# A residual gate's terms moved from three engines to GpSimd, and its closing matmul done by split products

## The chip, the cores and the metric

The kernel runs on one core of one Trainium2 chip. The metric is device time in microseconds (us) of one execution, the median of three runs. Five queues of instructions run side by side on the core: PE (TensorE, with PEld its weight loads), DVE (VectorE), ACT (ScalarE), POOL (GpSimd) and SP (SyncE, which issues most of the transfers). Each runs its own instructions in order; semaphores tie them together.

## The reference

One layer of a hybrid encoder over 1024 tokens of width 1024, in fp32:

```python
mod = silu(c) @ w_ada + b_ada                  # shift, scale, gate: 1024 each
u = layer_norm(x) * (1 + scale) + shift
h = u @ w_in                                   # q, k, v, g of 8 FoX and 8 stick-breaking heads
y_fox = fox_attention(...) * silu(fg)          # softmax with a forget bias, causal
y_sb = stick_breaking_attention(...) * silu(sg)
y = concat([y_fox, y_sb]) @ w_out
out = layer_norm(2**0.25 * x + gate * y, ln_g, ln_b)
```

Only `gate` matters here: `gate = silu(c) @ w_ada[:, 2048:] + b_ada[2048:]`, a vector of 1024 numbers. Value heads and `w_out` are drawn with a smaller scale (DeepNorm).

## The kernel before, in words

Products that need fp32 accuracy are split: a number is its fp32r part (hi) plus the rest (lo), and three fp32r matmuls (hi·hi, hi·lo, lo·hi) stand for one fp32 matmul. The weights are read from HBM in pieces of 128x512 (`raw`) and split on POOL by `fetch_w`: a TENSOR_SCALAR makes hi (L125), a TENSOR_TENSOR subtraction makes lo (L126).

The heads run in 8 pairs. The program begins with the first projections of pairs 0 and 1 (q, k, g of pair 0, q and k of pair 1): a first pass over tokens 0 to 511 and then a second pass over tokens 512 to 1023 (the loops at L740 and L752), eight blocks `kb` of 128 input channels each, accumulated in PSUM. `late_round` turns and rounds the inputs of the second pass. `evac_m` empties an accumulator: ACT casts, DVE subtracts, and for keys (`evac_k`) SP copies the head's half across partitions by DMA (L243). The last accumulator of the second pass is `st_k1b`, keys of pair 1.

After that attention goes unit by unit: a unit is a pair p, a head h and a query block i. `att_scores` multiplies queries and keys (S, L411 and L412, one buffer); for stick-breaking heads ACT makes two sigmoids out of it (`kp`, `be`, L431 and L432), DVE runs a cumulative product over `kp` (the scan, L437 and L441), POOL multiplies (L445). Two units later `att_transpose` turns `be` (T, L462), and ACT and DVE split the result (`pt`, L464 and L465). `att_pv` multiplies by the values (L477). Between these PE works through a list of fillers, first the remaining value tiles of pairs 0 and 1 (`v_tile`, L311 to L313) and the g projection of pair 1.

The gate: the 1024 rows of its weight come in eight tiles `wg` of 128x1024 (`load_gate`), in the buffers of the tag `att` (six of them, shared with inputs `x`, with `kp` and `be`, and with the bias tile `bg`). `gate_term` scales a tile by silu(c) of its rows (`sc`) and adds it to `gate`, in two halves of 512 columns. Here ACT makes the first term and scales the left halves, POOL adds these, and DVE does the right halves in one instruction. `gen_gate` then adds up the 128 partitions by a plain fp32 matmul with a matrix of 0.5 and adds half of the bias (DVE, L717). It runs beside the first fillers and waits GATE of their steps. The result is used only much later, when POOL multiplies it into `w_out` (L123).

What sets the order: PE and, in the start, SP run in the order in which the program text issues them. ACT, DVE and POOL are ordered by a planner, which places each instruction when its own clock says that it can run; buffers of a tag go to the next tile when their last reader is done. So where the text issues the gate's work decides the order of SP and, through the planner, that of the others.

Of the kernel before, what the change touches and what calls it, by code (L numbers as in the profile page):

```python
# [8 lines left out]
F32 = mybir.dt.float32  # L9
F32R = mybir.dt.float32r  # L10
AF = mybir.ActivationFunctionType
ALU = mybir.AluOpType

P = 128
SEQ = 1024
D = 1024
NB = 8
# [10 lines left out]
def tile_hybrid_layer(  # L28
# [17 lines left out]
    nc = tc.nc  # L46

    cp = ctx.enter_context(tc.tile_pool(name="const", bufs=1))
# [4 lines left out]
    def big(tag, bufs, name, dt=F32, shape=None):  # L53
        return sb.tile(shape or [P, 1024], dt, tag=tag, bufs=bufs, name=name)

    def att_tile(name, dt=F32):
        return big("att", 6, name, dt)

    def pt_tile(which, name, dt=F32R, shape=None):
        return big("pth" if which == 0 else "ptl", 3, name, dt, shape)  # L60

    def acc_tile(name):
        return ps.tile([P, 512], F32, tag="acc", bufs=2, name=name)
# [4 lines left out]
    def t_tile(name):  # L68
        return ps.tile([P, 512], F32, tag="T", bufs=2, name=name)
# [3 lines left out]

    RING = 5
    WARM = (4, 1, 1, 1, 1)
    GEARLY = 8
    NORM_ON = {6: nc.vector, 7: nc.vector}
    FROW = 12
    SPACE = 5
    GATE = 6  # L80

    def after(*instructions):
        stack = ExitStack()
        for i in instructions:
            stack.enter_context(tc.issue_after(i.ins))
        return stack
# [7 lines left out]
                            channel_multiplier=1, compare_op=ALU.is_ge, fill=MASKED)  # L94
    ones = cp.tile([P, 1], F32, tag="ones", name="ones")
    nc.gpsimd.memset(ones, 1.0)
    half = cp.tile([P, 1], F32, tag="half", name="half")
    nc.gpsimd.memset(half, 0.5)

    qz = [[cp.tile([P, P], F32R, tag=f"qz{h}{b}", name=f"qz{h}{b}") for b in range(2)] for h in range(2)]  # L100
    for h in range(2):
# [2 lines left out]
    gate = cp.tile([P, D], F32, tag="gate", name="gate")  # L104
# [8 lines left out]
    def raw_tile(name):  # L113
        return sb.tile([P, 528], F32, tag="wraw", bufs=2, name=name)

    def ring_w(key):
        return [sb.tile([P, 528], F32R, tag=tag, bufs=RING, name=f"{tag}_{key}") for tag in ("whi", "wlo")]

    def fetch_w(key, src, n, scale=None, home=None):
        raw = raw_tile(f"raw_{key}")[:, :n]  # L120
        nc.sync.dma_start(raw, src)
        if scale is not None:
            nc.gpsimd.tensor_tensor(raw, raw, scale, op=ALU.mult)  # L123
        hi, lo = home or ring_w(key)
        nc.gpsimd.tensor_scalar(hi[:, :n], raw, 1.0, 1.0, op0=ALU.mult, op1=ALU.mult)  # L125
        nc.gpsimd.tensor_tensor(lo[:, :n], raw, hi.bitcast(F32)[:, :n], op=ALU.subtract)  # L126
        return hi, lo
# [30 lines left out]
    sc = cp.tile([P, NB], F32, tag="sc", name="sc")  # L158
# [3 lines left out]
    for kt in range(NB):  # L162
        nc.tensor.matmul(sc_all[:, kt // 4, kt % 4 * P:][:, :P], sc[:, kt:kt + 1].to_broadcast([P, P]), ident,
                         start=True, stop=True)
# [52 lines left out]
    def u_round(kb, a=0, b=512):  # L217
        full = xT[kb, a][:, :b - a]
        nc.scalar.activation(u_hi[kb][:, a:b], full, AF.Identity, scale=modc[:, kb, 0:1], bias=modc[:, kb, 1:2])
        return nc.scalar.activation(full, full, AF.Identity, scale=modc[:, kb, 0:1], bias=modc[:, kb, 1:2])  # L220
# [340 lines left out]
    def start_steps(ns, accs, kb, a=0, b=512, parts=(0, 1)):  # L561
        s = slice(a, b)
        w = {}
        for n in ns:
            hi, lo = split[("k", kb) if n < NW else ("h", kb // 4)]
            at = n if n < NW else kb % 4
            w[n] = hi[:, at * P:at * P + P], lo[:, at * P:at * P + P]
        if 0 in parts:
            for n in ns:
                nc.tensor.matmul(accs[n], w[n][0], u_hi[kb][:, s], start=(kb == 0), stop=False)  # L570
                nc.tensor.matmul(accs[n], w[n][1], u_hi[kb][:, s], start=False, stop=False)
        if 1 in parts:
            for n in ns:
                nc.tensor.matmul(accs[n], w[n][0], u_lo[kb][:, s], start=False, stop=(kb == NB - 1))
# [36 lines left out]
    rounded = u_round(0)  # L611
# [14 lines left out]
    v0_w, v0_raw = {}, {}  # L626
# [63 lines left out]
    wg = {}  # L690

    def load_gate(kt):
        wg[kt] = att_tile(f"wg_{kt}")
        nc.sync.dma_start(wg[kt], w_gate[kt])

    def gate_term(kt, h):
        s = slice(h * 512, h * 512 + 512)
        if kt == 0:
            nc.scalar.activation(gate[:, s], wg[kt][:, s], AF.Copy, scale=sc[:, 0:1])
        elif h == 0:  # L700
            nc.scalar.activation(wg[kt][:, s], wg[kt][:, s], AF.Copy, scale=sc[:, kt:kt + 1])
            nc.gpsimd.tensor_tensor(gate[:, s], gate[:, s], wg[kt][:, s], op=ALU.add)
        else:
            nc.vector.scalar_tensor_tensor(gate[:, s], wg[kt][:, s], sc[:, kt:kt + 1], gate[:, s],
                                           op0=ALU.mult, op1=ALU.add)

    def gen_gate():
        b = att_tile("bg")
        nc.sync.dma_start(b, b_gate.to_broadcast([P, D]))
        for _ in range(GATE):  # L710
            yield
        for h in range(2):
            s = slice(h * 512, h * 512 + 512)
            gp = t_tile(f"gate_{h}")

            nc.tensor.matmul(gp, half.to_broadcast([P, P]), gate[:, s], start=True, stop=True)
            nc.vector.scalar_tensor_tensor(gate[:, s], b[:, s], 0.5, gp, op0=ALU.mult, op1=ALU.add)  # L717
            yield

    def late_round(kb):  # L720
        u_turn(kb, 512, 1024)
        return u_round(kb, 512, 1024), u_rest(kb, 512, 1024)
# [13 lines left out]
    rounded = late_round(1)  # L736
# [3 lines left out]
    for kb in range(NB):  # L740
        if kb + 2 < NB:
            rounded = late_round(kb + 2)
        start_steps(range(2), acc1, kb, 512, 1024)
        if kb < 4:
            load_gate(kb)
        if kb < len(evacs):
            n, h = evacs[kb]
            with after(*rounded):
                evac_m(*START[n], 0, acc0[n], (h,))
    acc1 += [pv_tile("st_g0b", True), pv_tile("st_q1b"), acc_tile("st_k1b")]  # L750
    v0_w.update((n, fetch_w(f"v0_{n}b", w_v[0, n], 512)) for n in (2, 3))
    for n in range(5):  # L752
        if n >= 2:
            for kb in range(NB):
                start_steps((n,), acc1, kb, 512, 1024)
                step = (n - 2) * NB + kb
                if step % 3 == 1 and step // 3 < GEARLY:
                    with after(*rounded):
                        gate_term(step // 3, 0)
                        gate_term(step // 3, 1)  # L760
                    if step // 3 < 4:
                        load_gate(step // 3 + 4)
        last_evac = evac_m(*START[n], 1, acc1[n])
        if n == 2:
            floor.append(ps.tile([P, 512], F32, tag="fl", bufs=1, name="floor"))
            nc.vector.memset(floor[0][:, :512 - P], 0.0)
            nc.scalar.copy(floor[0][:, 512 - P:], ident)
# [184 lines left out]
    for k in range(len(units) + LAG + 1):  # L952
        if k < len(units):
# [12 lines left out]
            p, h, i = units[k]  # L966
# [85 lines left out]
```

## Time and profile before

| | us |
|---|---|
| median of 3 runs | 694.79 |
| lowest, highest | 694.29, 694.94 |
| the profiled execution | 694.61 |
| its span, first to last instruction | 692.6 |
| PE busy in the span | 674.5 (97%) |
| DVE, ACT, POOL busy | 462.3, 384.3, 410.1 |

The profiled execution took 694.61 us, of which 692.6 us lie between the first and the last instruction; some 2.0 us are around it. The granted TensorE clock was 0.996 on average. In the profile's rows a line number is that of the kernel before, a name is a tile's with the buffer numbers left out, and what stands in brackets is the idle time ahead of an instruction and what ended it.

### The profile page before, as it was taken

Reading aid. Unit: us, or ns where it says so; the run is one execution under the profiler, and the core shown is the slowest. Engines: PE = TensorE matmul, PEld = TensorE weight load, DVE = VectorE, ACT = ScalarE, POOL = GpSimd, SP = SyncE. Lnnn points to the kernel's source line nnn. Section 1 sums busy time; section 2 is a strip of 40 time slices with the busy share of each in tenths; the row PEclk is TensorE's granted clock in tenths of the full one; section 3 lists DMA queues with packets and bytes.
Section 4 is the critical chain, followed back from the end, with each engine's and each line's share of the span. In section 5 each row is a group of like instructions: output and inputs, shape, how many; then the busy total and the mean of one; then the engine's idle time right before and its main releaser. Section 6 shows DMA issues by size and latency. Waiting matters only on the chain.

```text
span 692.6 us, 11784 instructions
## 1 busy us (share of the span) xinstructions
PE 674.5 (97%) x4033; PEld 589.2 (85%) x4033; DVE 462.3 (67%) x930; ACT 384.3 (55%) x866; POOL 410.1 (59%) x532
## 2 busy tenths in 40 slices
PE   7999999999999999999999999999999999999995
PEld 4789888888998888889998888889988889888884
DVE  5985668776656676767576665666565667774644
ACT  4666557766658576666675564655565667521000
POOL 4560477565439565556388897877584364655422
PEclk9999999999999999999999999999999999999998
DMA  8953351102102112112044553454341298153301
GB/s 308 415 228 129 95 196 55 28 23 55 54 9 70 41 48 60 38 46 62 12 142 156 176 161 114 146 159 145 100 130 58 75 293 339 58 170 108 118 31 61
DMA packets 44027, 81.59 MB, mean 118 GB/s; under 512 B 5120, under 2 KB 18880, under 8 KB 43072
## 3 DMA queue, kind: packets, MB, share of 16 engines
q1 hardware_dynamic: 42816, 76.65, 33.5%
q10 hardware_dynamic: 1152, 4.19, 2.1%
q8 instruction: 32, 0.52, 0.3%
q14 instruction: 27, 0.22, 0.1%
HBM read 60.34 MB, written 16.29 MB: 111 GB/s over the span
## 4 chain that ended last, share of the span: by engine, by line
PE 86%; DVE 5%; DMA 3%; ACT 3%; POOL 2%; issue 1%; SPq 0%; POOLq 0%; DVEq 0%; ACTq 0%
PE m L256 10%; PE m L257 10%; PE m L258 10%; PE pv L477 10%; PE T L462 9%; PE S L412 5%; PE S L411 5%; PE o L838 4%; PE o L836 4%; PE o L837 4%; PE v L311 4%; PE v L313 4%; PE v L312 4%; DMA wss<-in_w_ss_dram 1%; DMA x<-in_x_dram 1%
## 5 line engine op out<-in xcount | busy, mean ns | idle before, releaser
L256 PE MATMUL m<-uh,whi 128*128 128x512 f32 x304 | 126.4, 416 | 0.5 <-DVE kl L244 0.5
L257 PE MATMUL m<-ul,whi 128*128 128x512 f32 x304 | 119.8, 394 | 0.0
L258 PE MATMUL m<-uh,wlo 128*128 128x512 f32 x304 | 119.6, 394 | 0.0
L465 DVE TENSOR_TENSOR pt<-T,pt 128x512 fp32r<-128x512 f32 (+2 forms) x192 | 100.6, 550 | 18.4 <-ACT pt L464 17.2
L445 POOL TENSOR_TENSOR be<-be,kp 128x127 f32<-128x127 f32 (+3 forms) x64 | 77.1, 1205 | 33.7 <-DVE kp L441 25.0
L464 ACT CAST pt<-T 128x512 fp32r<-128x512 f32 (+2 forms) x192 | 85.7, 480 | 17.6 <-PE T L462 13.9
L437 DVE TENSOR_TENSOR_SCAN kp<-kp,floor 128x512 f32<-128x512 f32 (+2 forms) x64 | 65.1, 1018 | 33.6 <-ACT kp L431 32.5
L477 PEld LDWEIGHTS pv<-pt,v 128*128 128x128 f32 (+1 forms) x640 | 77.3, 163 | 4.8 <-DVE pt L465 0.6
L477 PE MATMUL pv<-pt,v 128*128 128x256 f32 (+3 forms) x640 | 80.8, 272 | 0.4 <-DVE pt L465 0.4
L426 POOL TENSOR_SCALAR a<-a,l 128x1024 f32<-128x1024 f32 (+3 forms) x64 | 47.9, 748 | 38.6 <-DVE l L425 25.1
L258 PEld LDWEIGHTS m<-uh,wlo 128*128 128x128 f32 x304 | 57.1, 188 | 13.5
L424 ACT ACTIVATE a<-a,nm 128x1024 f32<-128x1024 f32 (+3 forms) x64 | 49.8, 778 | 33.8 <-DVE nm L418 33.3
L411 PE MATMUL S<-k,q 128*128 128x512 f32 (+5 forms) x192 | 66.6, 348 | 0.7 <-ACT be L432 0.5
L412 PE MATMUL S<-kl,qz 128*128 128x512 f32 (+5 forms) x192 | 65.5, 342 | 0.0
L256 PEld LDWEIGHTS m<-uh,whi 128*128 128x128 f32 x304 | 57.3, 188 | 9.2 <-DVE kl L244 0.9
L257 PEld LDWEIGHTS m<-ul,whi 128*128 128x128 f32 x304 | 57.4, 189 | 8.0
L498 POOL TENSOR_TENSOR ty<-ty,sg 64x256 f32<-64x256 f32 x64 | 47.5, 741 | 25.9 <-DVE ty L497 12.8
L418 DVE CUSTOM_DVE_ANT_0 a<-S,fb 128x1024 f32<-128x1024 f32 (+3 forms) x64 | 48.3, 755 | 20.3 <-PE S L412 10.0
L431 ACT ACTIVATE kp<-S 128x128 f32<-128x128 f32 (+3 forms) x64 | 41.7, 651 | 31.9 <-PE S L412 28.6
L311 PE MATMUL v<-whi_v,uh 128*128 128x256 f32 (+1 forms) x192 | 56.0, 292 | 0.7 <-DVE kl L244 0.7
L389 ACT CAST qz<-q 64x128 fp32r<-64x128 f32 x128 | 37.3, 295 | 32.7 <-PE S L412 31.6
L313 PE MATMUL v<-wlo_v,uh 128*128 128x256 f32 (+1 forms) x192 | 54.2, 282 | 0.0
(286 smaller groups left out, 1606.4 us busy)
## 6 DMA issues: line engine op xcount, KB each, us to landing
raw<-in_w_qkg_dram SPq DMA_DIRECT2D x38, 256.0 KB, 2.9
wss<-in_w_ss_dram SPq DMA_DIRECT2D x7, 1024.0 KB, 8.5
x<-in_x_dram SPq DMA_DIRECT2D x8, 512.0 KB, 7.5
k<-k SPq DMA_DIRECT2D x32, 128.0 KB, 2.4
wg<-in_w_gate_dram SPq DMA_DIRECT2D x8, 512.0 KB, 5.0
raw_o<-in_w_out_dram SPq DMA_DIRECT2D x16, 256.0 KB, 2.8
fb<-f_dr ACTq DMA_DIRECT2D x8, 512.0 KB, 4.2
wo_dr<-whi_o SPq DMA_DIRECT2D x16, 256.0 KB, 2.4
```

Source lines behind the costliest of these rows:

```text
L256: nc.tensor.matmul(acc, hi[:, c], u_hi[kt][:, s], start=(kt == 0), stop=False)
L257: nc.tensor.matmul(acc, hi[:, c], u_lo[kt][:, s], start=False, stop=False)
L258: nc.tensor.matmul(acc, lo[:, c], u_hi[kt][:, s], start=False, stop=(kt == NB - 1))
L311: nc.tensor.matmul(acc[:, :n], u_hi[kt][:, ts_], hi[:, s], start=(kt == 0), stop=False)
L313: nc.tensor.matmul(acc[:, :n], u_hi[kt][:, ts_], lo[:, s], start=False, stop=(kt == NB - 1))
L411: nc.tensor.matmul(S[:, s, :w], qst[p][h][:, qs], kst[p][h][:, ks], start=True, stop=False)
L412: nc.tensor.matmul(S[:, s, :w], z, klo[p][:, ks], start=False, stop=True)
L437: scan = nc.vector.tensor_tensor_scan(rv, rv, floor[0][:, 512 - n:][:, ::-1], initial=0.0, op0=ALU.mult, op1=ALU.max)
L445: nc.gpsimd.tensor_tensor(be[:, :ke - 1], be[:, :ke - 1], kp[:, 1:ke], op=ALU.mult)
L464: nc.scalar.copy(hi[:, :n, qo:qo + P], t3)
L465: nc.vector.tensor_tensor(lo[:, :n, qo:qo + P], t3, hi.bitcast(F32)[:, :n, qo:qo + P], op=ALU.subtract)
L477: nc.tensor.matmul(acc[:m, q0:256], vt[p][:, kb, h * P:h * P + m], pt[:, kb % 4, q0:], start=start, stop=stop)
```

## The change

Four things. All gate terms run on POOL, a TENSOR_SCALAR for the scaling and a TENSOR_TENSOR for the sum, per half. They are issued inside the loop of the second pass over `kb`: terms 0 to 3 at kb = 0 to 3, and terms 4 to 7 with their loads all at kb = 3, together with the two value weights `v0_2b` and `v0_3b`; so all of these transfers stand on SP ahead of the keys' copies of pair 1's first half and pair 0's second half. The closing sum takes two fp32r matmuls per half, on a hi part cast by ACT and a lo part subtracted by POOL (two tiles of the tag `pth`). And it comes earlier, after 3 steps of the fillers in place of 6: on PE the two matmuls of the left half now stand right ahead of the scores of unit (0,0,2), those of the right half right ahead of the scores of unit (0,0,3).

```diff
@@ constants @@
-    GEARLY = 8
...
-    GATE = 6
+    GATE = 3
...
-    half = cp.tile([P, 1], F32, tag="half", name="half")
-    nc.gpsimd.memset(half, 0.5)
+    half = cp.tile([P, 1], F32R, tag="half", name="half")
+    nc.gpsimd.memset(half.bitcast(F32), 0.5)
...
     def gate_term(kt, h):
         s = slice(h * 512, h * 512 + 512)
         if kt == 0:
-            nc.scalar.activation(gate[:, s], wg[kt][:, s], AF.Copy, scale=sc[:, 0:1])
-        elif h == 0:
-            nc.scalar.activation(wg[kt][:, s], wg[kt][:, s], AF.Copy, scale=sc[:, kt:kt + 1])
+            nc.gpsimd.tensor_scalar(gate[:, s], wg[kt][:, s], sc[:, 0:1], 1.0, op0=ALU.mult, op1=ALU.mult)
+        else:
+            nc.gpsimd.tensor_scalar(wg[kt][:, s], wg[kt][:, s], sc[:, kt:kt + 1], 1.0, op0=ALU.mult, op1=ALU.mult)
             nc.gpsimd.tensor_tensor(gate[:, s], gate[:, s], wg[kt][:, s], op=ALU.add)
-        else:
-            nc.vector.scalar_tensor_tensor(gate[:, s], wg[kt][:, s], sc[:, kt:kt + 1], gate[:, s],
-                                           op0=ALU.mult, op1=ALU.add)
 
     def gen_gate():
         b = att_tile("bg")
         nc.sync.dma_start(b, b_gate.to_broadcast([P, D]))
+        parts = [pt_tile(0, f"gate_{x}") for x in range(2)]
+        nc.scalar.copy(parts[0], gate)
+        nc.gpsimd.tensor_tensor(parts[1], gate, parts[0].bitcast(F32), op=ALU.subtract)
         for _ in range(GATE):
             yield
         for h in range(2):
             s = slice(h * 512, h * 512 + 512)
             gp = t_tile(f"gate_{h}")
-
-            nc.tensor.matmul(gp, half.to_broadcast([P, P]), gate[:, s], start=True, stop=True)
+            for part in range(2):
+                nc.tensor.matmul(gp, half.to_broadcast([P, P]), parts[part][:, s], start=(part == 0), stop=(part == 1))
             nc.vector.scalar_tensor_tensor(gate[:, s], b[:, s], 0.5, gp, op0=ALU.mult, op1=ALU.add)
             yield
...
         start_steps(range(2), acc1, kb, 512, 1024)
         if kb < 4:
             load_gate(kb)
+            gate_term(kb, 0)
+            gate_term(kb, 1)
+        if kb == 3:
+            v0_w.update((n, fetch_w(f"v0_{n}b", w_v[0, n], 512)) for n in (2, 3))
+            for kt in range(4, NB):
+                load_gate(kt)
+                gate_term(kt, 0)
+                gate_term(kt, 1)
...
-    v0_w.update((n, fetch_w(f"v0_{n}b", w_v[0, n], 512)) for n in (2, 3))
     for n in range(5):
         if n >= 2:
             for kb in range(NB):
                 start_steps((n,), acc1, kb, 512, 1024)
-                step = (n - 2) * NB + kb
-                if step % 3 == 1 and step // 3 < GEARLY:
-                    with after(*rounded):
-                        gate_term(step // 3, 0)
-                        gate_term(step // 3, 1)
-                    if step // 3 < 4:
-                        load_gate(step // 3 + 4)
```

Three places show how the order moves. In these rows a line number is that of the kernel in question (the same statement has a number smaller by one in the changed kernel, up to `gate_term`), names carry pair, head and block, and the brackets name the queues that an instruction waits for.

POOL, from the second half of the value weights (`whi_v0_2b`, `wlo_v0_2b`) to the first unit's product `be_0_0_0`; `whi_1_2_0` and its like are the weights of pair 1's g projection. Before:

```order
L125 TENSOR_SCALAR whi_v0_2b_803<-raw_v0_2b_801 128x512 [waits DMAHW6_49,PE_49]
L125 TENSOR_SCALAR whi_v0_3b_809<-raw_v0_3b_807 128x512 [waits DMAHW7_49,PE_49]
L126 TENSOR_TENSOR wlo_v0_2b_804<-raw_v0_2b_801,whi_v0_2b_803 128x512 [waits Pool_49]
L126 TENSOR_TENSOR wlo_v0_3b_810<-raw_v0_3b_807,whi_v0_3b_809 128x512 [waits Pool_49]
L702 TENSOR_TENSOR gate_88<-gate_88,wg_4_831 128x512 [waits DMAHW2_49,Activation_49]
L702 TENSOR_TENSOR gate_88<-gate_88,wg_5_845 128x512 [waits DMAHW3_49,Activation_49,Pool_49]
L702 TENSOR_TENSOR gate_88<-gate_88,wg_6_859 128x512 [waits DMAHW4_49,Activation_49,Pool_49]
L125 TENSOR_SCALAR whi_1_2_0_1224<-raw_1_2_0_1222 128x512 [waits DMAHW6_49,PE_49]
L702 TENSOR_TENSOR gate_88<-gate_88,wg_7_878 128x512 [waits DMAHW5_49,Activation_49,Pool_49]
L125 TENSOR_SCALAR whi_1_2_1_1230<-raw_1_2_1_1228 128x512 [waits DMAHW7_49,PE_49]
L126 TENSOR_TENSOR wlo_1_2_0_1225<-raw_1_2_0_1222,whi_1_2_0_1224 128x512 [waits Pool_49]
L126 TENSOR_TENSOR wlo_1_2_1_1231<-raw_1_2_1_1228,whi_1_2_1_1230 128x512 [waits Pool_49]
```

And now:

```order
L124 TENSOR_SCALAR whi_v0_2b_768<-raw_v0_2b_766 128x512 [waits DMAHW4_49,PE_49]
L124 TENSOR_SCALAR whi_v0_3b_774<-raw_v0_3b_772 128x512 [waits DMAHW5_49,PE_49]
L701 TENSOR_TENSOR gate_88<-gate_88,wg_7_796 128x512 [waits Pool_49]
L125 TENSOR_TENSOR wlo_v0_2b_769<-raw_v0_2b_766,whi_v0_2b_768 128x512 [waits Pool_49]
L125 TENSOR_TENSOR wlo_v0_3b_775<-raw_v0_3b_772,whi_v0_3b_774 128x512 [waits Pool_49]
L708 TENSOR_TENSOR gate_1_968<-gate_88,gate_0_967 128x1024 [waits DVE_49,Activation_49]
L124 TENSOR_SCALAR whi_1_2_0_1237<-raw_1_2_0_1235 128x512 [waits DMAHW6_49,PE_49]
L124 TENSOR_SCALAR whi_1_2_1_1243<-raw_1_2_1_1241 128x512 [waits DMAHW7_49,PE_49]
L125 TENSOR_TENSOR wlo_1_2_0_1238<-raw_1_2_0_1235,whi_1_2_0_1237 128x512 [waits Pool_49]
L125 TENSOR_TENSOR wlo_1_2_1_1244<-raw_1_2_1_1241,whi_1_2_1_1243 128x512 [waits Pool_49]
L445 MEMSET be_0_0_0_958 128x1 [waits Activation_49]
L444 TENSOR_TENSOR be_0_0_0_958<-be_0_0_0_958,kp_0_0_0_957 128x127 [waits DVE_49]
```

All 30 instructions of the gate's terms (16 scalings, 14 sums) now stand ahead of the value weights but for the last sum, and the subtraction L708 stands between the value weights and pair 1's; before, three sums stood ahead of the value weights and four behind.

ACT, around the evacuation of the second pass's last accumulators. Before:

```order
L701 ACTIVATE wg_4_831<-wg_4_831,sc_100 128x512 [waits DMAHW2_49]
L232 ACTIVATE q_1_0_251<-st_q1b_799 64x512 [waits PE_49]
L701 ACTIVATE wg_5_845<-wg_5_845,sc_100 128x512 [waits DMAHW3_49]
L232 ACTIVATE q_1_1_252<-st_q1b_799 64x512 [waits DVE_49]
L701 ACTIVATE wg_6_859<-wg_6_859,sc_100 128x512 [waits DMAHW4_49,Activation_49]
L701 ACTIVATE wg_7_878<-wg_7_878,sc_100 128x512 [waits DMAHW5_49,Pool_49]
L241 CAST k_1_0_253<-st_k1b_800 64x512 [waits PE_49]
L389 CAST qz00_80<-q_0_0_246 64x128 [waits PE_49]
L241 CAST k_1_1_254<-st_k1b_800 64x512 [waits DVE_49]
```

And now:

```order
L231 ACTIVATE q_1_0_251<-st_q1b_849 64x512 [waits PE_49]
L707 CAST gate_0_967<-gate_88 128x1024 [waits Pool_49]
L231 ACTIVATE q_1_1_252<-st_q1b_849 64x512 [waits DVE_49]
L240 CAST k_1_0_253<-st_k1b_850 64x512 [waits PE_49]
L388 CAST qz00_80<-q_0_0_246 64x128 [waits PE_49]
L240 CAST k_1_1_254<-st_k1b_850 64x512 [waits DVE_49]
```

The four scalings are gone, and one cast of the finished gate stands there, which waits for POOL. On DVE the four right halves that stood among the same evacuations are gone as well.

SP, the transfers after the first four gate tiles. Before:

```order
L243 DMA k_1_0_253<-k_1_0_253 64x512 [waits DMAHW4_49,Activation_49,Pool_49]
L243 DMA k_1_1_254<-k_1_1_254 64x512 [waits DMAHW5_49,Activation_49,Pool_49]
L121 DMA raw_v0_2b_801<-in_w_v_dram 128x512 [waits DMAHW6_49]
L121 DMA raw_v0_3b_807<-in_w_v_dram 128x512 [waits DMAHW7_49]
L243 DMA k_0_0_248<-k_0_0_248 64x512 [waits DMAHW0_49,Activation_49]
L243 DMA k_0_1_249<-k_0_1_249 64x512 [waits DMAHW1_49,Activation_49]
L694 DMA wg_4_831<-in_w_gate_dram 128x1024 [waits DMAHW2_49,PE_49]
L694 DMA wg_5_845<-in_w_gate_dram 128x1024 [waits DMAHW3_49,DVE_49,PE_49]
L694 DMA wg_6_859<-in_w_gate_dram 128x1024 [waits DMAHW4_49]
L694 DMA wg_7_878<-in_w_gate_dram 128x1024 [waits DMAHW5_49,DVE_49,Pool_49]
L121 DMA raw_1_2_0_1222<-in_w_qkg_dram 128x512 [waits DMAHW6_49,Pool_49]
```

And now:

```order
L120 DMA raw_v0_2b_766<-in_w_v_dram 128x512 [waits DMAHW4_49]
L120 DMA raw_v0_3b_772<-in_w_v_dram 128x512 [waits DMAHW5_49]
L693 DMA wg_4_778<-in_w_gate_dram 128x1024 [waits DMAHW6_49,DMAHW0_49,Pool_49]
L693 DMA wg_5_784<-in_w_gate_dram 128x1024 [waits DMAHW7_49,DMAHW1_49,Pool_49]
L693 DMA wg_6_790<-in_w_gate_dram 128x1024 [waits DMAHW2_49,Pool_49]
L693 DMA wg_7_796<-in_w_gate_dram 128x1024 [waits PE_49]
L242 DMA k_1_0_253<-k_1_0_253 64x512 [waits Activation_49]
L242 DMA k_1_1_254<-k_1_1_254 64x512 [waits DMAHW3_49,Activation_49]
L242 DMA k_0_0_248<-k_0_0_248 64x512 [waits DMAHW4_49,Activation_49]
L242 DMA k_0_1_249<-k_0_1_249 64x512 [waits DMAHW5_49,Activation_49]
L120 DMA raw_1_2_0_1235<-in_w_qkg_dram 128x512 [waits DMAHW6_49,Pool_49]
```

The six weight transfers stand ahead of the four key copies, and three of the gate tiles now wait for POOL, whose earlier terms free their buffers.

## The prediction

> **What bounds the kernel now.** I read the page's engine shares first, then busy time by stretch, then PE's waits around the place of the change.
>
> ```profile
> PE 674.5 (97%) x4033; PEld 589.2 (85%) x4033; DVE 462.3 (67%) x930; ACT 384.3 (55%) x866; POOL 410.1 (59%) x532
> ```
>
> ```profile
> core 0: us, PE busy (x) PEld busy (x) DVE busy (x) ACT busy (x) POOL busy (x), PEclk, DMA share, GB/s
> 56.00:75.00 19.00, 19.00 (x121) 16.71 (x120) 10.29 (x19) 16.09 (x28) 0.00 (x0) 1.00 0.31 107
> 75.00:92.00 17.00, 17.00 (x75) 13.71 (x73) 11.41 (x14) 7.63 (x14) 11.26 (x9) 1.00 0.53 182
> 108.00:120.00 12.00, 10.73 (x75) 9.23 (x74) 11.02 (x17) 8.99 (x20) 9.80 (x12) 1.00 0.21 57
> 200.00:300.00 100.00, 100.00 (x599) 87.98 (x598) 67.42 (x108) 66.10 (x144) 63.44 (x88) 1.00 0.17 48
> ```
>
> PE is the bound: 97% of the span, and full from 56 to 92 us, where the second pass runs, and again from 200 to 300. A gap closed before PE fills up again therefore shortens the kernel by its own length, and work taken off DVE or ACT inside 56 to 92 us buys nothing there. POOL does nothing at all from 56 to 75 us. PE has its holes between 92 and 120 us, behind the second pass; by PE's timeline these, with the scores of units 1, 2 and 5 for what follows:
>
> ```profile
> 95.19 0.28 PE L313 MATMUL v<-wlo_v_3b,uh 128*128 128x256 f32 x1
> 96.00 0.39 PE L411 MATMUL S<-k,q 128*128 128x256 f32 x1 [0.53 <-ACT be L432]
> 96.34 0.30 PE L311 MATMUL v<-v_home,uh 128*128 128x256 f32 x1
> 97.80 0.34 PE L411 MATMUL S<-k,q 128*128 128x384 f32 x1
> 97.98 0.34 PE L412 MATMUL S<-kl,qz 128*128 128x384 f32 x1
> 99.43 0.33 PE L462 MATMUL T<-ident,be 128*128 128x128 f32 x1 [1.11 <-POOL be L446]
> 106.66 0.42 PE L411 MATMUL S<-k,q 128*128 128x384 f32 x1
> 115.74 0.84 PE L462 MATMUL T<-ident,be 128*128 128x128 f32 x6 [0.86 <-DVE pt L465]
> ```
>
> The gate's work is behind the first two. ACT and DVE, in the same stretch:
>
> ```profile
> 91.44 1.34 ACT L701 ACTIVATE wg<-wg,sc 128x512 f32<-128x512 f32 x2
> 92.80 0.58 ACT L241 CAST k<-st_k1b 64x512 fp32r<-64x512 f32 x1
> 94.89 0.58 ACT L241 CAST k<-st_k1b 64x512 fp32r<-64x512 f32 x1 [1.32 <-DVE kl L244]
> 95.67 0.27 ACT L432 ACTIVATE be<-S 128x128 f32<-128x128 f32 x1
> ```
>
> ```profile
> 92.54 1.60 DVE L704 SCALAR_TENSOR_TENSOR gate<-wg,sc,gate 128x512 f32<-128x512 f32 x1
> 94.17 0.68 DVE L244 TENSOR_TENSOR kl<-st_k1b,k 64x512 fp32r<-64x512 f32 x1
> 95.51 0.69 DVE L244 TENSOR_TENSOR kl<-st_k1b,k 64x512 fp32r<-64x512 f32 x1 [0.65 <-ACT k L241]
> ```
>
> **The change part by part.** (1) The first hole. `st_k1b` is emptied in four steps by turns, ACT, DVE, ACT, DVE, and unit 0's sigmoids come behind them on ACT. The chain is late because ACT scales `wg` until 92.78 and DVE holds a gate term until 94.14, though the first cast ended at 93.38. Without both, the first cast starts when PE is done:
>
> ```profile
> 92.00 0.39 PE L574 MATMUL st_k1b<-ul,hw 128*128 128x512 f32 x1
> ```
>
> That is at 92.45, 0.35 sooner, and the DVE wait of 94.17 − 93.40 = 0.77 goes: everything behind is 1.12 earlier, `be` of unit 0 read at 94.82 in place of 95.94, the last `kl` done at 95.08 in place of 96.20. PE comes to the scores of unit 1 at 95.19 + 0.12 = 95.31 and needs the first of these, then 0.24 later a new accumulator, which needs the second. Both are there. The value tile then starts at 95.55 instead of 96.34: **0.79 us**.
>
> (2) The second hole: T of unit 0 waits for POOL's product `be`, which stands behind POOL's splits of pair 1's weights, and those behind the last gate sums.
>
> ```profile
> 75.32 4.72 POOL L702 TENSOR_TENSOR gate<-gate,wg 128x512 f32<-128x512 f32 x3 [23.32 <-ACT wg L701]
> 93.56 1.06 POOL L125 TENSOR_SCALAR whi<-raw 128x512 fp32r<-128x512 f32 x1
> 96.42 2.55 POOL L126 TENSOR_TENSOR wlo<-raw,whi 128x512 fp32r<-128x512 f32 x2
> ```
>
> Behind S at 97.98 + 0.18 = 98.16 PE was free, T began at 99.43: 1.27 us. Whether that goes depends on POOL's new chain, which has to be added up, from the first gate tile's landing to the product:
>
> ```profile
> 52.70 1.97 SPq L694 DMA_DIRECT2D wg<-in_w_gate_dram  x4
> DMA to landing us min/median/max: 3.9/5.0/6.6
> L702 POOL TENSOR_TENSOR gate<-gate,wg x7: 1284/1309/1634, 75.3 to 94.6; 128x512 f32<-128x512 f32 x7
> L704 DVE SCALAR_TENSOR_TENSOR gate<-wg,sc,gate x7: 751/1276/1723, 74.7 to 92.5; 128x512 f32<-128x512 f32 x7
> L125 POOL TENSOR_SCALAR whi<-raw 128x512 fp32r<-128x512 f32 x38 | 23.9, 630 | 13.5 <-DMA raw<-in_w_qkg_dram 6.6 <-PE m L257 3.3 <-PE pv L477 2.1
> L126 POOL TENSOR_TENSOR wlo<-raw,whi 128x512 fp32r<-128x512 f32 x38 | 49.1, 1295 | 3.1 <-DMA wo_dr<-wlo_o 1.6
> L426 POOL TENSOR_SCALAR a<-a,l 128x512 f32<-128x512 f32 x8 | 5.5, 692 | 5.3 <-DVE l L425 5.3
> L445 POOL TENSOR_TENSOR be<-be,kp 128x1023 f32<-128x1023 f32 x8 | 16.0, 1999 | 4.4 <-DVE kp L441 4.4
> ```
>
> Start: 52.70 + 3.9 = 56.6. Sixteen scalings cost between 16·0.63 = 10.1 (L125) and 16·0.69 = 11.1 (L426, which has the same form, a column of factors); fourteen sums 14·1.284 = 18.0; the value weights' split 2·0.63 + 2·1.295 = 3.85; the subtraction L708 between 2.0 (L445) and twice L126, 2.6; pair 1's split 3.85; the product 0.4. Sum 38.2 to 39.8, end at 94.8 to 96.4. In the new program PE asks for it at 95.55 + 1.46 (the half value tile, 96.34 to 97.80) + 0.47 (two gate matmuls, below) + 0.36 (two score matmuls) = 97.84. So POOL has 1.4 to 3.0 us in hand, and the hole closes: **1.27 us**. POOL can also wait for its tiles: wg_4 to wg_6 are freed by its own terms, wg_7 by PE's last turn of x at about 71.2. With landings of 3.9 none is late; with 6.6, wg_7 comes at 77.8 where POOL, by the sum, wants it at about 76, and 1.7 of the reserve is spent. Each is issued with no other transfer beside it, so I take the short landing.
>
> [...] The undisturbed rows above, 1284 against 751 ns, say 1.7 times. [...]
>
> (3) The closing sum. The chain of waits has what one fp32 matmul (two passes) takes on PE's path, and PE's timeline how closely fp32r matmuls of 128x512 follow each other, 0.23 us:
>
> ```profile
> 105.31 0.86 PE gate L716 x2
> ```
>
> ```profile
> 77.78 0.40 PE L571 MATMUL st_g0b<-uh,wlo_st 128*128 128x512 f32 x1
> 78.01 0.39 PE L574 MATMUL st_g0b<-ul,whi_st 128*128 128x512 f32 x1
> ```
>
> Two halves: 2·(0.86 − 2·0.23) = **0.80 us**. ACT's new cast of 128x1024 (at most two halves like L701's above, 1.34) runs behind the gate's end, which by the sum above is some 10 us before POOL's product, at 85 to 87; ACT is wanted at 92.45, so POOL would have to be 4 us late to push it into that.
>
> (4) The transfers on SP. The key copies now stand behind wg_7, which waits for PE's last turn of x, some 20 us before the scores of unit 4 need the second half: no cost. `raw_1_2` now waits for the value weights' split, about 88 to 89, and lands 3 us later, as POOL comes to it. The new close one is `bg`: L716 on DVE needs it, stands ahead of the scan of unit 2, and frees the PSUM tile that the right half's matmul takes at 99.43.
>
> ```profile
> 94.05 0.45 SPq L709 DMA_DIRECT2D bg<-in_b_gate_dram  x1
> bg<-in_b_gate_dram SPq DMA_DIRECT2D x1, 512.0 KB, 4.2
> ```
>
> It follows the key copy of the first cast, so 0.35 sooner: 93.70 + 4.2 = 97.9, L716 (0.67, as the 0.68 of L244 above) done at 98.6, 0.8 before PE asks. I cost it at nothing; landing after 6.6 it would cost 1.6.
>
> From unit 2 on I carry PE's own steps: scores of unit 5 came at 106.66 and now 0.79 + 1.27 − 0.92 + 0.86 = 2.0 sooner, both gate sums being done by then; those of unit 6 another 0.86 sooner. ACT then starts unit 6's sigmoid 2.9 us sooner, and DVE, which sets the pace from there to 119 (11.02 of 12 us busy), keeps that lead with its hole of 0.86 at 115.74 in it. DVE also loses L717's two additions there, but the sigmoid's end sets DVE's start, so I count nothing for them. Sum: 0.79 + 1.27 + 0.80 = **2.9 us**. The profiled execution goes from a span of 692.6 to 689.7, and with its 2.0 around it to 691.7; it lay 0.18 under the median, so against 694.79 I predict 691.9.
>
> **The rivals.** First, the hand-over stalls anew (chance 0.16): POOL or `bg` is some 1.5 to 2 us late, T or the right half's matmul waits, and the gain is 0.8 to 1.5 us: about 693.6. For it: DVE and ACT now carry the gate's end in their busiest corner, with 0.8 us in hand. Against: in the trace transfers issued alone landed in 3.9 to 4.2.
>
> Second, nothing arrives (0.12): the holes at 96 and 99 us are those of any start of attention (one S buffer, sigmoid, scan, product), and only the matmul's 0.80 is left: 694.0. For it: later starts of units have similar waits. Against: the 1.60 of L704 and the 1.34 of L701 stand right in the chain.
>
> Third, the loser (0.11): POOL's chain is slowed by DVE. POOL's sums took up to 1634 ns and one TENSOR_SCALAR 1.06 us while DVE ran L704. If all thirty are like that, POOL ends 14·0.35 + 16·0.43 = 11.8 us later, near 107; T at 97.84 waits 9 to 10, and the kernel takes about 702. It decides from some 1.4 + 2.9 = 4.3 us of delay, 0.14 per instruction; ACT's cast, waiting for the gate, would hold the evacuations too. Against it: the slow ones all stand beside L704, which goes, and the splits at 82 to 86 beside DVE's evacuations took
>
> ```profile
> 83.28 1.30 POOL L126 TENSOR_TENSOR wlo_v_2b<-raw_v_2b,whi_v_2b 128x512 fp32r<-128x512 f32 x1
> ```
>
> [...]
>
> **How the numbers follow.** The forecast has 0.61; its own range is 691.0 to 693.0 (0.9 more where DVE's hole closes, 1.1 less where most of one hole stays). With the first two rivals the range is 690.7 to 694.5. A measurement of this kernel tells about 0.2%, 1.4 us, from no change. Faster by that: the forecast, and 0.6 of the first rival, 0.70; same: the rest of it, the second and a little of the third's edge, 0.19; slower 0.11.
>
> **What would show it.** Right: POOL busy from about 57 to 96 us without sums above 1.35 us; no wait of scores of unit 1 on ACT; T of unit 0 without a wait; the first cast of `st_k1b` at 92.45; gate matmuls at 0.23 each; PE's later rows all 2.9 us sooner. Wrong: T's wait on POOL stays; PE waits at the right half's matmul for L716; the gate's cast on ACT starts after 91; PE has new holes between 56 and 92.

## The result, and the profile after

The changed kernel takes 691.81 us (median of 5 runs, 691.02 to 692.37) where the kernel before takes 694.64 (694.29 to 694.94): a ratio of 0.9959 with a 95% interval of 0.9948 to 0.9970, 2.8 us less. The prediction was 691.9, against 694.79 for the kernel before, the median of the first three of these five runs. The profiled execution took 691.02 us with a span of 689.3.

The rows below are PE's timeline of the changed kernel, where the prediction looked for its holes; line numbers are now those of the changed kernel, one less than before around attention (L410 was L411, L461 was L462).

```profile
91.70 0.22 PE L410 MATMUL S<-k,q 128*128 128x128 f32 x1
94.78 0.28 PE L410 MATMUL S<-k,q 128*128 128x256 f32 x1
95.01 0.28 PE L310 MATMUL v<-v_home,uh 128*128 128x256 f32 x1
96.44 0.62 PE L715 MATMUL gate<-gate,half 128*128 128x512 f32 x2
96.89 0.34 PE L410 MATMUL S<-k,q 128*128 128x384 f32 x1
97.24 0.27 PE L461 MATMUL T<-ident,be 128*128 128x128 f32 x1
98.79 0.62 PE L715 MATMUL gate<-gate,half 128*128 128x512 f32 x2
112.24 0.85 PE L461 MATMUL T<-ident,be 128*128 128x128 f32 x6 [0.78 <-DVE pt L464]
116.61 0.93 PE L461 MATMUL T<-ident,be 128*128 128x128 f32 x7
```

Neither the scores of unit 1 (94.78) nor T of unit 0 (97.24) have a wait in brackets any more; the wait of T for DVE at 112.24 stayed, 0.78 in place of 0.86. The first row is the scores of unit 0. The same two ends of the stretch in the kernel before:

```profile
92.23 0.22 PE L411 MATMUL S<-k,q 128*128 128x128 f32 x1
119.96 0.93 PE L462 MATMUL T<-ident,be 128*128 128x128 f32 x7
```

From the scores of unit 0 to T of unit 6 (seven matmuls) PE took 119.96 − 92.23 = 27.73 us before and takes 116.61 − 91.70 = 24.91 now: 2.82 less. From there to the end of the span both take the same: 692.6 − 119.96 = 572.6 and 689.3 − 116.61 = 572.7. The other 0.53 by which the two spans differ lies ahead of the change's place: the first value tile of the stage before the second pass starts at 51.96 and 51.43, ahead of the first gate tile's transfer. So the stretch, called **S0 to T6** below, is the finer measure. In all thirteen profiles of this study what follows it took 572.6 to 572.8 us. No kernel was profiled twice, but the step from the scores of unit 0 to those of unit 1 is 3.07 or 3.08 us in all eleven profiles in which no hole stands there.

POOL, by its timeline from the first gate tile to unit 0's product, with the groups of its two gate lines between 50 and 110 us (shapes, count, busy us and mean ns, idle time before):

```profile
56.23 1.37 POOL L698 TENSOR_SCALAR gate<-wg,sc 128x512 f32<-128x512 f32 x2 [4.75 <-DMA wg<-in_w_gate_dram]
88.26 2.39 POOL L708 TENSOR_TENSOR gate<-gate,gate 128x1024 fp32r<-128x1024 f32 x1
94.33 0.10 POOL L445 MEMSET be<- 128x1 f32 x1
95.07 0.41 POOL L444 TENSOR_TENSOR be<-be,kp 128x127 f32<-128x127 f32 x1 [0.64 <-DVE kp L436]
```

```profile
L701 POOL TENSOR_TENSOR gate<-gate,wg 128x512 f32<-128x512 f32 x14 | 17.8, 1288 | 0.0
L700 POOL TENSOR_SCALAR wg<-wg,sc 128x512 f32<-128x512 f32 x14 | 9.4, 686 | 0.0
```

POOL runs without a gap from 56.23 to 94.43, and then it waits for DVE's scan, so POOL no longer holds up the attention. Busy time by stretch shows where the work went:

```profile
56.00:75.00 19.00, 19.00 (x118) 16.63 (x117) 9.72 (x17) 14.48 (x25) 18.77 (x22) 1.00 0.60 217
75.00:92.00 17.00, 17.00 (x76) 13.75 (x75) 5.20 (x8) 5.44 (x10) 17.00 (x17) 1.00 0.19 46
```

PE stays full for both stretches of the second pass, DVE falls from 11.41 to 5.20 us between 75 and 92, and POOL fills 56 to 92.

### The profile page after: what moved, and what is told of

Its sections match the earlier page's. It is cut to its first block, busy times and chain, and to the rows that moved or that the text cites. A ratio compares the mean times of both kernels' runs of the same rounds, so it can differ in the third digit from the quotient of the medians.

```text
span 689.3 us, 11785 instructions
## 1 busy us (share of the span) xinstructions
PE 673.6 (98%) x4033; PEld 589.7 (86%) x4033; DVE 453.9 (66%) x923; ACT 379.8 (55%) x858; POOL 430.4 (62%) x556
## 5 line engine op out<-in xcount | busy, mean ns | idle before, releaser
L410 PE MATMUL S<-k,q 128*128 128x512 f32 (+5 forms) x192 | 66.5, 348 | 0.2 <-DVE nm L417 0.2
L411 PE MATMUL S<-kl,qz 128*128 128x512 f32 (+5 forms) x192 | 65.5, 342 | 0.0
```

Source lines behind the costliest of these rows:

```text
L410: nc.tensor.matmul(S[:, s, :w], qst[p][h][:, qs], kst[p][h][:, ks], start=True, stop=False)
L411: nc.tensor.matmul(S[:, s, :w], z, klo[p][:, ks], start=False, stop=True)
```

## The experiments

The table has all medians, their ratios to the kernel before (with 95% intervals) and, from each kernel's profile, S0 to T6. The kernels ran in four groups, each with its own executions of the kernel before, and a ratio is to those. Their medians were 694.64 (the change), 694.65 (no gate, plain sum, split sum, POOL alone), 694.30 (sum later, three engines, 2 and 6 passes) and 694.34 (3 and 4 passes, rounded sum), so medians of different groups compare to no better than some 0.3 us.

| kernel | median us | ratio to before | S0 to T6, us | against before |
|---|---|---|---|---|
| before | 694.64 | | 27.73 | |
| the change | 691.81 | 0.9959 [0.9948, 0.9970] | 24.91 | −2.82 |
| no gate at all | 690.71 | 0.9944 [0.9931, 0.9957] | 24.01 | −3.72 |
| plain closing sum | 692.63 | 0.9971 [0.9960, 0.9981] | 25.71 | −2.02 |
| closing sum later | 691.50 | 0.9956 [0.9944, 0.9967] | 24.78 | −2.95 |
| split sum alone | 695.91 | 1.0023 [1.0014, 1.0033] | 29.11 | +1.38 |
| POOL alone | 696.90 | 1.0036 [1.0022, 1.0050] | 30.25 | +2.52 |
| early place, three engines | 699.30 | 1.0063 [1.0049, 1.0077] | 27.54 | −0.19 |
| POOL 2 passes later | 691.63 | 0.9962 [0.9950, 0.9973] | 25.12 | −2.61 |
| 3 passes | 693.19 | 0.9984 [0.9976, 0.9993] | 26.58 | −1.15 |
| 4 passes | 696.72 | 1.0036 [1.0024, 1.0048] | 29.85 | +2.12 |
| 6 passes | 700.85 | 1.0092 [1.0079, 1.0105] | 34.00 | +6.27 |
| rounded sum, later | 691.78 | 0.9962 [0.9950, 0.9975] | 25.20 | −2.53 |

The theory is the prediction's: three separate gains (a hole at the scores of unit 1, a hole at T of unit 0, a cheaper matmul), all of them on condition that POOL is done before PE asks for T. Its rivals: only one of the parts pays, or the gate still costs something elsewhere.

**The ceiling.** The gate is left out.

```diff
+    nc.gpsimd.memset(gate, 1.0)
...
     def gen_gate():
-        b = att_tile("bg")
...
+        return
```

> The gate left out of the computation altogether: the gate's tile is set to 1.0 at the start, its weights and bias are not loaded, and there are no terms, no closing sum and no addition of the bias. This is the ceiling. My theory: the changed kernel has no wait left that the gate causes, so only its four matmuls go, 0.93 us, and the rest of PE's row stands: 0.9 us less than the changed kernel, 3.7 less than before. Rival, that the gate's work still costs PE waits elsewhere (DVE's additions in the stretch to 119 us, transfers, POOL's 38 us): more than 1.5 us less than the changed kernel.

S0 to T6 is 0.90 shorter than with the change, and the median 1.1. So what the gate still costs there agrees with its four matmuls: 0.93 expected, 0.90 found. The rival of a further cost, 1.5 us and more, is out.

**The closing sum.** The changed kernel with the fp32 matmul put back:

```diff
-        parts = [pt_tile(0, f"gate_{x}") for x in range(2)]
-        nc.scalar.copy(parts[0], gate)
-        nc.gpsimd.tensor_tensor(parts[1], gate, parts[0].bitcast(F32), op=ALU.subtract)
...
+            nc.tensor.matmul(gp, half.to_broadcast([P, P]), gate[:, s], start=True, stop=True)
```

> The changed kernel with the closing sum as it was before: one fp32 matmul for each half, no cast and no subtraction. By my theory (three separate gains, 0.79 and 1.27 us by the two holes and 0.80 us by the split products) the two gate matmuls take 0.86 us each again in place of two pairs of 0.24, so the kernel takes 0.8 us more than the changed one, 2.0 us less than before; scores of unit 1 and T of unit 0 still wait for nothing. Rival, that the holes are hidden again by what follows and only the split products pay: it is back within 0.3 us of before. Rival, that the split products are hidden (DVE, which sets the pace of units 3 to 6, takes up the 0.8 us): same as the changed kernel, 2.8 us less than before.

S0 to T6 is 0.80 longer than with the change, the median 0.82. The price of the two fp32 matmuls comes back whole, and nothing more: T and the scores of unit 1 have no wait in this kernel either. DVE does not take the 0.8 us up.

The other way round, the split sum in the kernel before:

```diff
+        parts = [pt_tile(0, f"gate_{x}") for x in range(2)]
+        nc.scalar.copy(parts[0], gate)
+        nc.gpsimd.tensor_tensor(parts[1], gate, parts[0].bitcast(F32), op=ALU.subtract)
```

> The kernel before with the split closing sum alone: the gate's terms stay on ACT, POOL and DVE at their old places. My theory: the split costs a cast on ACT (1.0 us) and a subtraction on POOL (2.4 us), and at the old place both stand in the late corner, the cast between the two evacuations of st_k1b, the subtraction ahead of POOL's product for unit 0. T of unit 0 then waits some 2.4 us longer than its 1.1 of before, against 0.8 saved on PE: 1.5 to 2.6 us more than before. Rival, that split products are worth 0.8 us wherever they stand: 0.8 us less than before.

Slower, by 1.38 in S0 to T6 and 1.26 in the median, a little less than the 1.5 to 2.6 I gave. The place isn't what I expected either. PE and ACT of this kernel:

```profile
91.90 0.22 PE L411 MATMUL S<-k,q 128*128 128x128 f32 x1
97.64 0.39 PE L411 MATMUL S<-k,q 128*128 128x256 f32 x1 [2.50 <-ACT be L432]
101.28 0.33 PE L462 MATMUL T<-ident,be 128*128 128x128 f32 x1 [1.34 <-POOL be L446]
```

```profile
95.46 1.04 ACT L711 CAST gate<-gate 128x1024 fp32r<-128x1024 f32 x1 [2.29 <-POOL gate L702]
96.53 0.58 ACT L241 CAST k<-st_k1b 64x512 fp32r<-64x512 f32 x1
```

I had put the loss at T. It is at the scores of unit 1: ACT's cast waits 2.29 us for POOL's last gate sum and holds the second evacuation of `st_k1b` behind it. That hole grows by 1.97 (from the scores of unit 0: 97.64 − 91.90 = 5.74 against 96.00 − 92.23 = 3.77), T's step by 0.21, the matmuls give 0.80: +1.38, as found. So the split products don't pay where the gate is done late; with the change, where it is done early, they are worth 0.80.

**POOL without the early place.** The kernel before with the new `gate_term`:

```diff
-            nc.scalar.activation(wg[kt][:, s], wg[kt][:, s], AF.Copy, scale=sc[:, kt:kt + 1])
...
-            nc.vector.scalar_tensor_tensor(gate[:, s], wg[kt][:, s], sc[:, kt:kt + 1], gate[:, s],
-                                           op0=ALU.mult, op1=ALU.add)
+            nc.gpsimd.tensor_scalar(wg[kt][:, s], wg[kt][:, s], sc[:, kt:kt + 1], 1.0, op0=ALU.mult, op1=ALU.mult)
+            nc.gpsimd.tensor_tensor(gate[:, s], gate[:, s], wg[kt][:, s], op=ALU.add)
```

> The kernel before with one part of the change: every gate term on POOL (a scaling and a sum for each half), at the old place in the program, with the old order of transfers and the fp32 closing sum. My theory: POOL gets 14 scalings and 7 sums more, some 18 us, all from 75 us on, when the old place issues the terms, so POOL ends its gate work some 10 us later than before, near 105; T of unit 0 waits for the product that stands behind it, and the kernel takes 4 to 10 us more than before. Rival, that what pays is to free ACT and DVE of the terms: first hole gone, 0.8 us less than before, and the second no longer than it was.

Slower by 2.25 in the median and 2.52 in S0 to T6, which is less than the 4 to 10 us I gave: the planner lets unit 0's product go ahead of the last four gate sums. PE, POOL and ACT:

```profile
92.84 0.22 PE L411 MATMUL S<-k,q 128*128 128x128 f32 x1
95.92 0.28 PE L411 MATMUL S<-k,q 128*128 128x256 f32 x1
100.17 0.46 PE L411 MATMUL S<-k,q 128*128 128x384 f32 x1 [2.43 <-ACT be L432]
100.75 0.42 PE L462 MATMUL T<-ident,be 128*128 128x128 f32 x1
```

```profile
96.73 1.35 POOL L702 TENSOR_TENSOR gate<-gate,wg 128x512 f32<-128x512 f32 x1
99.23 0.48 POOL L445 TENSOR_TENSOR be<-be,kp 128x127 f32<-128x127 f32 x1
99.60 1.34 POOL L702 TENSOR_TENSOR gate<-gate,wg 128x512 f32<-128x512 f32 x1
```

```profile
99.74 0.38 ACT L432 ACTIVATE be<-S 128x256 f32<-128x256 f32 x1 [1.24 <-POOL be L445]
```

The first hole is closed here: the scores of unit 1 come 95.92 − 92.84 = 3.08 us after those of unit 0, as in the changed kernel (94.78 − 91.70 = 3.08) and not 3.77. So the first term needs only ACT and DVE to be free (both were freed together; what either alone would do was not tried). But unit 0's product is done at 99.71, ACT's sigmoid of unit 1 waits for POOL, and the hole of 2.43 us opens one step before T, at the scores of unit 2. The lower clock behind that hole (0.62 and 0.53 in the two windows from 100 to 104 us) adds to the loss (see the last section).

**The early place without POOL.** The changed kernel with the old `gate_term` (the diff above, reversed).

> The changed kernel's early place, order of transfers and closing sum, but the gate's terms shared by ACT, POOL and DVE as before. Tells whether it is the place or the engine that pays. My theory: both. ACT gets nine scalings of 0.67 us, 6.0 us, between 56 and 75 us, where it is busy for 14.5 of 19 us in the changed kernel with the tiles that PE's second pass needs; it has at most 4.5 us left there, so PE gets holes of 1.5 to 4 us in the second pass, while both old holes behind it stay closed: 1.5 to 4 us more than the changed kernel. Rival, that the early place alone pays: within 0.3 us of the changed kernel.

It took 699.30, 7.5 us more than the change, where I gave 1.5 to 4 (in its profiled execution, 697.82, it is 6.8; the six executions spread from 696.36 to 699.70). Two things happen. First the second pass, by the stretches of this kernel and two rows of its PE, the last turn of `x` and the scores of unit 0:

```profile
56.00:75.00 19.00, 17.58 (x110) 14.54 (x110) 13.74 (x23) 18.35 (x33) 9.43 (x7) 1.00 0.61 225
```

```profile
73.61 0.66 PE L212 MATMUL xT<-ident,x 128*128 128x128 f32 x4 [0.71 <-DVE ul L222]
95.74 0.22 PE L410 MATMUL S<-k,q 128*128 128x128 f32 x1
```

ACT is busy for 18.35 of 19 us and PE only for 17.58. The scores of unit 0 come 4.0 us later than with the change; 0.9 of that is there before the second pass (its first value tile ahead of it starts at 52.31, with the change at 51.43), so the second pass costs some 3.2, within what I gave for it. Then, behind it, the gate's bias, which I had not seen coming:

```profile
98.99 0.33 SPq L708 DMA_DIRECT2D bg<-in_b_gate_dram  x1
104.45 0.69 DVE L719 SCALAR_TENSOR_TENSOR gate<-bg,gate 128x512 f32<-128x512 f32 x1 [3.79 <-DMA bg<-in_b_gate_dram]
105.19 0.72 PE L718 MATMUL gate<-gate,half 128*128 128x512 f32 x2 [2.21 <-DVE gate L719]
```

`bg` is issued 3.3 us after the scores of unit 0 (with the change 1.3) and lands 5.3 us after its issue, not 4.2; the addition waits for it, and PE waits for the addition's PSUM tile. This is the prediction's first rival, in a kernel in which SP is later. So POOL can't be left out of the change. The early place by itself, with the old closing sum and the old order of transfers, was not run.

**The place of the closing sum.** One number: GATE = 6 in place of 3.

> The changed kernel with the closing sum at the place it had before, three steps of attention later (one number, 3 to 6). My theory: POOL's chain, the evacuation chain and the four matmuls stay as they are, the place is worth nothing: within 0.3 us of the changed kernel, 2.8 less than before. Rival, that the early place is part of the gain (its matmuls fill a hole of PE): up to 0.9 us more than the changed kernel.

S0 to T6 is 0.13 shorter, the median 0.3 lower, as is that of the kernel before beside it; the intervals overlap almost wholly. The place is worth nothing that can be told.

**POOL's reserve.** The changed kernel with 2, 3, 4 or 6 more passes on POOL; the diff is the same but for the number.

```diff
+            if kb == 2:
+                for _ in range(2):
+                    nc.gpsimd.tensor_scalar(gate, gate, 1.0, 1.0, op0=ALU.mult, op1=ALU.mult)
```

> The changed kernel with two passes more on POOL (the gate's sum multiplied by 1.0, 128x1024 each, some 1.1 us) behind the third term: POOL 2.3 us later, with nothing else changed. In the changed kernel POOL is done with all that stands ahead of unit 0's product at 94.43, the product itself waits for DVE's scan and ends at 95.48, and PE asks for T at 97.24. My theory: a reserve of about 2.4 us, so the product ends at about 97.1, and the kernel takes 0 to 0.3 us more than the changed one. Rival, that POOL's end passes straight on (no reserve): 1.2 to 2.3 us more.

> As the kernel with two extra passes on POOL, with three: POOL 3.4 us later. POOL's order has unit 0's product last, behind the subtraction and the split of pair 1's weights, so it ends at about 98.2, where PE asks for T at 97.24. My theory: about 1.0 us more than the changed kernel, as a wait of T for POOL. Rival, that the reserve is as short as the two passes: 1.2 us and more on top of theirs.

> With four extra passes, POOL 4.5 us later. POOL's order now has unit 0's product ahead of the subtraction, which ends at about 99.4, where PE wants it for the closing sum's second product at 96.7. My theory: a hole of 2.7 us at the gate's matmul, so about 2.7 us more than the changed kernel, as fast as before: the point from which the losing rival of the prediction decides. If PE's clock falls behind a hole of this length as it did in some of the earlier kernels, 1.5 us more, 4.2 in all. The two cases are told apart by the granted clock and by the spacing of the value tile's matmuls, 0.12 or 0.21 us.

> The changed kernel with six such passes more on POOL, 6.8 us. POOL's order then has the products of units 0 and 1 ahead of the subtraction for the closing sum. My theory: unit 0's product ends near 98.0, the subtraction at about 102; PE has the closing sum's second product ahead of the scores of unit 2 and of T, and wants it at 96.7, so PE waits there some 5.5 us: the kernel takes 4.5 to 7 us more than the changed one, 2 to 4 us more than before, and the wait is at the gate's matmul, not at T. Rival, that POOL's delay is hidden by the attention units behind: under 1.5 us more than the changed kernel.

In S0 to T6 these cost 0.21, 1.67, 4.94 and 9.09 us more than the change. The waits of PE between 50 and 200 us (line, what it waited for, us in total, times, longest) with three, four and six passes, those for POOL and ACT:

```profile
PE T L461 <- POOL be L445: 0.8, 1, 0.8
...
PE gate L715 <- POOL be L445: 0.3, 1, 0.3
```

```profile
PE gate L715 <- POOL be L445: 3.1, 1, 3.1
```

```profile
PE gate L715 <- POOL gate L708: 4.2, 1, 4.2
PE gate L715 <- ACT gate L707: 1.7, 1, 1.7
```

With two passes there is none: the product ends at 97.41 and PE asks for T at 97.68, so the reserve of about 2.4 us is real and nearly used up. With three passes T waits as I expected, and so does the gate's matmul beside it, since POOL's subtraction is late too: 1.67 for an expected 1.0. With four and six passes the wait is at the gate's matmul, as expected, but it costs more than I gave, 4.94 for 2.7 or 4.2 and 9.09 for 4.5 to 7. Two things make it dear. The passes don't only delay POOL, they change the planner's order. With four of them the subtraction stands behind unit 0's product and pair 1's splits:

```profile
97.83 0.42 POOL L444 TENSOR_TENSOR be<-be,kp 128x127 f32<-128x127 f32 x1
98.20 2.35 POOL L708 TENSOR_TENSOR gate<-gate,gate 128x1024 fp32r<-128x1024 f32 x1
```

It ends at 100.55, with the change at 90.65: 9.2 us later against the scores of unit 0, for 4.5 us of passes. And behind the wait PE runs at half its clock (0.50 from 102 to 104 us). The windows of the kernel with four passes (the granted clock is the third column from the right):

```profile
100.00:102.00 2.00, 1.39 (x9) 1.31 (x10) 0.69 (x1) 0.51 (x2) 1.92 (x5) 0.99 0.08 20
102.00:104.00 2.00, 2.00 (x11) 1.90 (x10) 1.14 (x2) 0.95 (x4) 2.00 (x3) 0.50 0.00 0
104.00:106.00 2.00, 2.00 (x11) 1.60 (x10) 1.18 (x3) 0.74 (x3) 0.01 (x1) 0.66 0.56 131
106.00:108.00 2.00, 2.00 (x18) 2.00 (x17) 1.53 (x2) 1.24 (x5) 0.63 (x2) 1.00 0.00 0
```

By the steps between scores: from those of unit 1 to those of unit 2 PE takes 5.49 us where the change takes 2.11 (the hole, 3.38), and from there to those of unit 5 8.68 where it takes 7.14 (the clock, 1.54): 4.92 of the 4.94. With six passes it is 6.68 and 2.39.

**Half the products.** The later closing sum of the rounded gate alone:

```diff
-        nc.gpsimd.tensor_tensor(parts[1], gate, parts[0].bitcast(F32), op=ALU.subtract)
...
+            nc.tensor.matmul(gp, half.to_broadcast([P, P]), parts[0][:, s], start=True, stop=True)
```

> The changed kernel with the closing sum three steps later and of the rounded gate alone: the low part is left out of the computation, with its subtraction on POOL (2.4 us) and two of the four matmuls. My theory: only the two matmuls count, 0.46 us less than the kernel with the later sum, 0.4 to 0.5 less than the changed one: 691.2. Rival, that POOL's 2.4 us still cost something there: 0.8 us less and more.

No gain: 691.78, and S0 to T6 is 0.42 longer than with the later sum it is to be compared with. T waits again:

```profile
97.88 0.33 PE L461 MATMUL T<-ident,be 128*128 128x128 f32 x1 [0.43 <-POOL be L445]
```

```profile
96.15 1.31 POOL L125 TENSOR_TENSOR wlo<-raw,whi 128x512 fp32r<-128x512 f32 x1
97.40 0.42 POOL L444 TENSOR_TENSOR be<-be,kp 128x127 f32<-128x127 f32 x1
```

With POOL free 2.4 us sooner the planner takes the next weights' split ahead of unit 0's product. What the two matmuls are worth by themselves is therefore not shown. No version here that computes the gate beats the changed kernel by more than the intervals.

## Why the prediction was right

The sum was 2.9 us, and S0 to T6 gives 2.82, the medians 2.83.

The first hole, 0.79. The value tile behind the scores of unit 1 started 96.34 − 92.23 = 4.11 us after the scores of unit 0 and now starts 95.01 − 91.70 = 3.31 after them: 0.80. That the gate's work on ACT and DVE was the cause is shown by the POOL-alone kernel, which closes this hole, while the second only moves. The evacuation's first cast came where the prediction had it, at 92.45 less the 0.53 of the earlier start, and ACT's cast of the gate stood well ahead of it:

```profile
86.80 1.03 ACT L707 CAST gate<-gate 128x1024 fp32r<-128x1024 f32 x1
91.89 0.58 ACT L240 CAST k<-st_k1b 64x512 fp32r<-64x512 f32 x1 [3.44 <-PE st_k1b L573]
```

The second hole, 1.27. From the value tile to T it was 99.43 − 96.34 = 3.09 and is 97.24 − 95.01 = 2.23, with 0.45 of gate matmuls in it that were not there: 1.31. POOL's chain, the term with the widest bounds, came out near the low end: 38.2 us up to the product and 38.6 with the product's 0.41, for 38.2 to 39.8, with sums of 1288 ns for the 1284 taken, scalings of 686 ns between the two rows used, and a subtraction of 2.39 between 2.0 and 2.6. Its end without the wait for DVE, 94.43 + 0.41 = 94.84 (95.37 with the 0.53 of the earlier start put back), was to be 94.8 to 96.4. The reserve of 1.4 to 3.0 is 97.24 − 94.84 = 2.4 by these rows, and two extra passes fit into it while three do not.

The matmul, 0.80. When it is undone, 0.80 comes back in S0 to T6 and 0.82 in the median.

The order on SP at no cost: the first addition of the bias ran from 97.30, and PE asks for its PSUM tile at 98.79, 0.8 later, as worked out.

```profile
97.30 0.69 DVE L716 SCALAR_TENSOR_TENSOR gate<-bg,gate 128x512 f32<-128x512 f32 x1 [0.74 <-DMA bg<-in_b_gate_dram]
```

The stretch to 119 us kept the lead, and DVE's hole there stayed (0.78).

The rivals. The hand-over did not stall, but it is what a delay of POOL or SP brings, as the kernels with three passes and with the three engines show. "Nothing arrives" fell with the ceiling and with the kernel with the plain sum. The loser's premise failed: DVE no longer has a gate term beside POOL's sums, and these took 1276 to 1314 ns. (The row that the prediction showed against this rival overlaps a DVE evacuation for only some 0.3 us; it is these fourteen sums, beside DVE's evacuations from 59 to 82 us, that settle it.) Its point of decision, 4.3 us of delay, was too late: 3.4 us still leave the kernel faster than before (0.9984), but 4.5, which by it should cost 0.2, cost 2.1 in S0 to T6. The step that was mis-sized is "1.4 + 2.9", one us of loss for one of delay: PE wants the closing sum's subtraction ahead of T, the planner put it behind unit 0's product once POOL was that late, and a long hole costs clock as well (1.54 us of the 4.94 with four passes). The forecast did not hang on this step.

## What to carry to other kernels

Here the split sum alone lost 1.3 us, POOL alone 2.3, and the change without POOL 5, while the whole won 2.8: the early place needs an engine that is idle there, the slower engine (an undisturbed gate sum took 1284 ns on POOL in the kernel before, a gate term on DVE 751, the 1.7 times of the prediction) needs the early place, and the cheaper closing sum needs the gate to be done early. So add up the new chain on the receiving engine against the time at which PE asks for what stands behind it, and take that reserve as the condition for all other terms. Beyond the reserve don't count one us of loss for one of delay: where a planner orders the engine, the order changes too. A stretch between two fixed instructions of PE, with a constant remainder, tells apart some tenths of a us where medians of this kernel can't.

## What the runs showed of the hardware

A hole of PE can cost more than its length: with four passes the steps between scores lost 3.38 us to the hole and 1.54 to the clock behind it. Behind this hole, a wait of 3.1 us, the granted clock fell to 0.50, and so it did behind 1.7 and 4.2 close together (six passes); the value tile's matmuls then follow each other at 0.21 us in place of 0.12. With POOL alone, a hole of 2.43 us was enough, by its windows and two of these matmuls:

```profile
98.00:100.00 2.00, 0.00 (x0) 0.00 (x0) 0.69 (x1) 0.64 (x2) 2.00 (x5) 1.00 0.06 14
100.00:102.00 2.00, 1.82 (x8) 1.73 (x9) 0.21 (x1) 1.04 (x4) 2.00 (x2) 0.62 0.52 135
102.00:104.00 2.00, 1.75 (x10) 1.45 (x8) 0.92 (x2) 0.56 (x2) 2.00 (x5) 0.53 0.35 90
```

```profile
102.03 0.41 PE L313 MATMUL v<-wlo_v_2b,uh 128*128 128x256 f32 x1
102.24 0.41 PE L311 MATMUL v<-whi_v_3b,uh 128*128 128x256 f32 x1
```

How long the low clock lasts can be estimated from the windows, if the clock is taken as either 1.00 or 0.50 at each moment, which the windows themselves don't show: a window of 2 us with a mean of c has 4·(1 − c) us at half clock. With POOL alone that is 4·0.38 + 4·0.47 = 3.4 us, with four passes 4·(0.01 + 0.50 + 0.34) = 3.4, and with six passes, where four windows have 0.65, 0.50, 0.50 and 0.65, twice as much, 6.8. It need not begin in the hole: with POOL alone it begins some 0.3 us after PE has started again, with four passes some 1.4 us after.

The profile of the split sum alone, with holes of 2.50 and 1.34, shows a clock of 1.00 around them, but its ten executions had mean clocks of 0.991 to 0.998 and times of 695.21 to 697.71. The early place with three engines, with a hole of 2.21, is alike: four of its six executions had 0.994 and took 699.12 to 699.70, the other two 0.996 and 0.997 and took 696.36 and 697.82. Kernels with no hole above 1.1 us between 50 and 200 us (the change, three passes and five others) had 0.996 to 0.998, those with four passes 0.991 to 0.995. So in these runs no drop was seen behind holes of up to 1.1 us, and with holes of 2.2 to 2.5 us it comes, by the mean clocks, in some executions and not in others. What decides between them is not shown.
